# The bias of the attention's exponentials, 24 small products, on Pool instead of DVE

## The chip, the cores and the metric

The kernel runs on one core of a Trainium2 chip. A core has a matrix engine (TensorE; PE in the profile, its weight loads PEld), a vector engine (VectorE; DVE), a scalar engine (ScalarE; ACT), a general engine (GpSimd; Pool, or POOL) and a queue that issues transfers (SyncE; SP). Each works off its own list of instructions in the order in which they were issued, and waits where one needs a result of another engine. The metric is the device time of one execution in microseconds; the kernel before takes 1005.35 us, the median of three runs (1005.01 to 1005.65).

## The reference

The reference is a decoder of two layers over 256 tokens of width 1024, in float32. Each layer is half a SwiGLU feed-forward block, a mixer and another half block, each on a normalised input and added to the stream. The mixer of the first layer is a short gated convolution; that of the second is sparse attention with 16 heads of 64 in 4 groups, in three branches (compressed, selected, window) that share one set of keys and values. At 256 tokens there are only four blocks of 64, so every block is selected, and the selected branch and the window branch are plain causal attention with keys of their own:

```
logits = einsum("bghtd,bgtkd->bghtk", qc, ks) * scale
p_sel  = softmax(where(smask, logits, -1e30))
o_sel  = einsum("bghtk,bgtkd->bghtd", p_sel, vs)
logits = einsum("bghtd,bgkd->bghtk", qc, kw) * scale
p_win  = softmax(where(wmask, logits, -1e30))
out    = gc[0] * o_cmp + gc[1] * o_sel + gc[2] * o_win
```

Queries are normalised per head with a learned gain, gates are sigmoids. Nearly all of the arithmetic is in the eight big weight products of the four feed-forward blocks.

## The kernel before, in words

The stream h lies transposed in SBUF, features on partitions. All weights come in float32 through one queue into three buffers `raw`; ScalarE rounds each to `whi`, VectorE (for a few units Pool) computes the rest `wlo = raw - whi`, and TensorE multiplies with both. Units of such work follow one another: feed-forward, convolution, feed-forward, shared keys and values, feed-forward, attention, feed-forward.

In the attention (`nsa`), 24 steps, called heads below, run through six rounds `U` of four: a round is a pair of query tile and half, and each head makes a 128 x 512 tile of logits `S` for both branches (`qk`). For one head the chain is:

- TensorE writes S in PSUM (weights are the scaled keys `kth` and `kts`, with the mask added by a product with `identb`).
- VectorE takes the negated maxima `mx` of S, 2 or 4 groups per row (lines 1168 and 1172).
- `nb = mx * sc` is the bias of the exponentials, 128 x 2 or 128 x 4 elements; `sc` is the query's scale, which Pool made before by a power (`q_stat`, line 1082).
- ScalarE computes `P = exp(sc * S + nb)` in 2 or 4 instructions, with row sums (line 1180).
- VectorE inverts the sums (`pw`), Pool multiplies them with the gates, and then P (128 x 512) by them (`weight`, lines 1187 to 1196).
- TensorE transposes P into `pb` (`tr`, two banks of `psB`), ScalarE rounds it to `ph`, VectorE makes the rest `pl`, and TensorE multiplies both with the values into `pc` (`pv`), which VectorE and ScalarE add up in `t`.

`mx` and `nb` are tiles of the pool `work`, with two buffers each, so that those of a head reuse the place of those of two heads before. S has four banks. Between these steps stand the compressed branch (`cm`, `mc`), the last query projections (`S<-hg,whi`, `qs`) and, from the middle on, the output projection `wo` of the first half.

The order in which each engine gets its instructions isn't that of the code. `Plan` records all operations with their dependences, gives each a cost (`_cost`; a small product on `gp` costs more there than one on `ve`) and a lag between engines (`LATENCY`), and a list scheduler (`schedule`, `sweep`) makes one order for each engine, four passes back and forth; `replay` then issues all of it, which is why the profile names line 419 for every instruction. A change of one operation's engine so changes costs and lags, and the order around it.

Of the kernel before, what the change touches and what calls it, by code (L numbers as in the profile page):

```python
# [15 lines left out]
ALU = mybir.AluOpType  # L16
# [415 lines left out]
def program(plan, a, out, ones):  # L432
    pe, ac, ve, gp, sp = (Engine(plan, k, None) for k in ("pe", "act", "dve", "gp", "sp"))
# [22 lines left out]
    def tt(eng, o, x, y, op):  # L456
        eng.tensor_tensor(o, x, y, op)
# [584 lines left out]
    def nsa(nkey, gname, okey, ogains):  # L1042
        st = {}
# [28 lines left out]
        def q_stat(i):  # L1072
            if i in st["stats"]:
                return
            st["stats"].add(i)
            t = psC.tile([128, 2, 2], F32, name="pc")
            for q in range(2):
                pe.matmul(t[:, q], st["sq", i][:, q * 128:(q + 1) * 128], blk2, start=True, stop=True)
            x = work.tile([128, 2, 2], F32, name="s8")
            ve.scalar_tensor_tensor(x, t, 1.0 / 64, st["em"][:, :, None].to_broadcast([128, 2, 2]),  # L1080
                                    op0=ALU.mult, op1=ALU.add)
            tt(gp, st["sc", i // 4][:, i % 4], x, neghalf[:, :, None].to_broadcast([128, 2, 2]), ALU.pow)
# [63 lines left out]
        def qk(i, hh):  # L1146
            j, q, ab = U[i]
            if hh % 2 == 0:
                P[i, hh // 2] = st["pool"].tile([128, 2, 4, 128], F32, name="P", bufs=5)
            if hh == 0:  # L1150
                SUM[i] = work.tile([128, 4, 4], F32, name="psum_")
            S = wide["pool"].tile([128, 512], F32, name="S")
            for x in range(2):
                e, y, k = (ab, hh, x) if q else (hh // 2, hh % 2 * 2 + x, 0)
                q_stat(j * 4 + y)
                qs = st["qs", j * 4 + y, e][:, q * 128:(q + 1) * 128]
                Sx = S[:, x * 256:(x + 1) * 256]
                Sb = Sx.rearrange("p (a b) -> p a b", a=2)
                pe.matmul(Sb, qs, kth[k][e][:, :, j], start=True, stop=False)
                if k == q:  # L1160
                    pe.matmul(Sx, identb, mask2, start=False, stop=False)
                pe.matmul(Sb, qs, kts[k][e][:, :, j], start=False, stop=True)
            g = 2 if q else 4
            mx = work.tile([128, 4], F32, name="mx")[:, :g]
            nb = work.tile([128, 4], F32, name="nb")[:, :g]
            if q:
                Sv = S.rearrange("p (k b c) -> p b k c", b=2, k=2)
                ve.tensor_reduce(mx, Sv, axis=AX.XY, op=ALU.max, negate=True)
                tt(ve, nb, mx, st["sc", j][:, hh, q, ab:ab + 1].to_broadcast([128, 2]), ALU.mult)
            else:  # L1170
                Sv = S.rearrange("p (x b c) -> p x b c", x=2, b=2)
                ve.tensor_reduce(mx, S.rearrange("p (g c) -> p g c", g=4), axis=AX.X, op=ALU.max, negate=True)
                tt(ve, nb.rearrange("p (x b) -> p x b", b=2), mx.rearrange("p (x b) -> p x b", b=2),
                   st["sc", j][:, hh % 2 * 2:hh % 2 * 2 + 2, q, hh // 2, None].to_broadcast([128, 2, 2]), ALU.mult)
            for y in range(g):
                if q:
                    o, x, z, e = P[i, hh // 2][:, hh % 2, 2 * y:2 * y + 2], Sv[:, y], hh, ab
                else:
                    o, x, z, e = P[i, hh // 2][:, hh % 2, y], Sv[:, y // 2, y % 2], hh % 2 * 2 + y // 2, hh // 2
                ac.activation(o, x, AF.Exp, bias=nb[:, y:y + 1], scale=st["sc", j][:, z, q, e:e + 1],  # L1180
                              accum_out=SUM[i][:, hh, y:y + 1])
# [113 lines left out]
        def attention():  # L1295
# [26 lines left out]
            for n in range(max(events) + 1):  # L1322
                st["head"] = n
                if n < len(heads):
                    if n == 12:
                        assert st["qdone"]
                    qk(*heads[n])
                    yield
                if 1 <= n <= len(heads):
                    weight(*heads[n - 1])  # L1330
                for f, args in sorted(events.get(n, []), key=lambda e: e[0] is not pv):
                    f(*args)
                    yield
# [92 lines left out]
    for u, x, y in HEAD:  # L1426
        if u == "h":
            x, y = NPAR * (x > 0) + x * T, NPAR + y * T
# [141 lines left out]
```

## Time and profile before

| | |
|---|---|
| time, median of 3 | 1005.35 us (1005.01 to 1005.65) |
| profiled execution | 1006.19 us, span 1004.4 us |
| mean granted clock of TensorE | 0.998 of full speed |
| busy PE / PEld | 983.8 us (98%) / 859.4 us (86%) |
| busy DVE / ACT / POOL | 734.3 us (73%) / 586.1 us (58%) / 203.2 us (20%) |
| chain that ended last | PE 85%, DVE 7%, ACT 3%, issue 2%, POOL 2% |
| heads of the attention | first `mx` at 724.6 us, last `nb` at 778.0 us |

The page counts an engine as busy while one of its instructions runs; the chain that ended last follows back, from the end, what each instruction waited for. Times in rows are counted from the start of the span. All instructions of the attention have the same line, so they are told apart by the names of the tiles: `nb<-mx,sc` writes nb from mx and sc.

### The profile page before, as it was taken

The page shows a single profiled execution, that of the slowest core. Times are in us where ns is not written, and L with a number is a line of the kernel's source. Part 1 is how long each engine was busy: PE and PEld are TensorE (multiplying, and loading weights), DVE is VectorE, ACT ScalarE, POOL GpSimd, SP SyncE. Part 2 cuts the span into 40 slices and gives each one's busy share as a digit, 9 for nine tenths or more (in the row PEclk, how much of TensorE's full clock was granted, in tenths as well). Part 3 has the DMA queues.
Part 4 walks back from the last instruction along what each step waited for, and adds up shares of the span by engine and source line. Part 5 has one row for each costly group of instructions (what it writes and reads, how often), then busy time and mean ns, then how long its engine had stood idle before and what let it go on. Part 6 is the DMA issues. An engine that isn't in the chain of part 4 may idle for free.

```text
span 1004.4 us, 15242 instructions
## 1 busy us (share of the span) xinstructions
PE 983.8 (98%) x5792; PEld 859.4 (86%) x5792; DVE 734.3 (73%) x1110; ACT 586.1 (58%) x1049; POOL 203.2 (20%) x242
## 2 busy tenths in 40 slices
PE   8999999999999999999899999999998999999998
PEld 5888888888888888889778888888986888888887
DVE  6876766688796767677989776676799787676554
ACT  8665554454565555554687565554698765555442
POOL 2211111022221111111421111111477431111100
PEclk9999999999999999999999999999999999999999
DMA  8655455655565554557366554455510245554353
GB/s 281 236 204 176 162 173 181 210 175 186 206 209 181 196 186 153 173 193 264 132 212 226 196 205 165 138 200 192 197 43 11 93 174 186 192 185 156 128 198 107
DMA packets 31033, 177.83 MB, mean 177 GB/s; under 512 B 3440, under 2 KB 6000, under 8 KB 16112
## 3 DMA queue, kind: packets, MB, share of 16 engines
q1 hardware_dynamic: 30960, 176.86, 51.4%
q8 instruction: 45, 0.74, 0.3%
q14 instruction: 28, 0.23, 0.1%
HBM read 175.80 MB, written 1.05 MB: 176 GB/s over the span
## 4 chain that ended last, share of the span: by engine, by line
PE 85%; DVE 7%; ACT 3%; issue 2%; POOL 2%; DMA 1%; SPq 1%; ACTq 0%; DVEq 0%; POOLq 0%
PE pa L419 52%; PE pb L419 29%; PE S L419 2%; PE pc L419 2%; DVE wlo L419 2%; ACT whi L419 1%; DVE mx L419 1%; DVE hg L419 1%; DVE nb L419 1%; DMA px<-in_px_dram 1%; DVE pl L419 1%; SPq L419 1%; DVE px L419 1%; POOL rf L419 0%; DVE t L419 0%
## 5 line engine op out<-in xcount | busy, mean ns | idle before, releaser
L419 PE MATMUL pa<-hg,whi 128*128 128x512 f32 (+1 forms) x1568 | 538.9, 390 | 2.9 <-DVE hg L419 2.7
L419 DVE TENSOR_TENSOR wlo<-raw,whi 128x1024 fp32r<-128x1024 f32 (+4 forms) x383 | 412.3, 1092 | 164.2 <-ACT whi L419 162.7
L419 ACT CAST whi<-raw 128x1024 fp32r<-128x1024 f32 (+3 forms) x388 | 350.6, 927 | 196.2 <-issue 80.9
L419 PE MATMUL pa<-hg,wlo 128*128 128x256 f32 x1536 | 430.8, 281 | 0.1
L419 PEld LDWEIGHTS pa<-hg,whi 128*128 128x128 f32 x1568 | 291.6, 187 | 68.8 <-DVE hg L419 4.5
L419 PEld LDWEIGHTS pa<-hg,wlo 128*128 128x128 f32 x1536 | 290.3, 189 | 0.9 <-DVE wlo L419 0.7
L419 PE MATMUL pb<-gg,whi 128*128 128x512 f32 x704 | 244.1, 392 | 0.0
L419 PE MATMUL pb<-gg,wlo 128*128 128x256 f32 x704 | 195.6, 279 | 0.0
L419 PEld LDWEIGHTS pb<-gg,whi 128*128 128x128 f32 x704 | 131.6, 187 | 29.4
L419 POOL TENSOR_TENSOR g<-s,t 128x256 f32<-128x256 f32 x88 | 70.3, 799 | 414.3 <-ACT s L419 410.4
L419 PEld LDWEIGHTS pb<-gg,wlo 128*128 128x128 f32 x704 | 132.7, 188 | 0.3
L419 ACT ACTIVATE s<-t 128x256 f32<-128x256 f32 x88 | 36.8, 418 | 138.3 <-DVE t L419 138.3
L419 POOL TENSOR_TENSOR acc<-acc,sq 128x256 f32<-128x256 f32 x36 | 33.5, 932 | 177.6 <-ACT sq L419 177.0
L419 DVE TENSOR_TENSOR t<-pa,t 128x512 f32<-128x512 f32 x94 | 64.3, 684 | 3.6 <-ACT t L419 3.4
L419 DVE TENSOR_TENSOR t<-t,R 128x512 f32<-128x512 f32 x96 | 66.2, 689 | 0.1
L419 ACT COPY t<-pa 128x512 f32<-128x512 f32 x94 | 54.5, 579 | 2.8 <-PE pa L419 2.6
L419 PE MATMUL S<-hg,whi 128*128 128x256 f32 (+1 forms) x224 | 49.2, 302 | 1.8 <-DVE hg L419 1.3
L419 DVE SCALAR_TENSOR_TENSOR px<-pb,px 128x256 f32<-128x256 f32 x56 | 23.7, 423 | 34.3 <-PE pb L419 33.4
L419 PE MATMUL pb<-hg,whi 128*128 128x512 f32 (+1 forms) x144 | 48.2, 386 | 0.0
L419 DVE TENSOR_TENSOR gg<-g,gg 128x256 fp32r<-128x256 f32 x88 | 37.2, 424 | 12.2 <-ACT gg L419 12.2
L419 ACT CAST gg<-g 128x256 fp32r<-128x256 f32 x88 | 35.4, 403 | 13.6 <-POOL g L419 12.5
L419 DVE SCALAR_TENSOR_TENSOR hg<-px,hg 128x256 fp32r<-128x256 f32 x56 | 39.6, 726 | 2.2 <-ACT hg L419 2.1
(176 smaller groups left out, 879.9 us busy)
## 6 DMA issues: line engine op xcount, KB each, us to landing
raw<-in_wgu_dram SPq DMA_DIRECT2D x86, 1024.0 KB, 4.8
raw<-in_wdn_dram SPq DMA_DIRECT2D x64, 704.0 KB, 4.1
raw<-in_wci_dram SPq DMA_DIRECT2D x8, 1024.0 KB, 5.0
raw<-in_wci_dram SPq DMA_DIRECT2D x8, 512.0 KB, 3.6
raw<-in_wco_dram SPq DMA_DIRECT2D x4, 1024.0 KB, 4.7
raw<-in_wkt_dram SPq DMA_DIRECT2D x4, 1024.0 KB, 4.8
raw<-in_wc_dram SPq DMA_DIRECT2D x4, 1024.0 KB, 4.9
raw<-in_wq_dram SPq DMA_DIRECT2D x4, 1024.0 KB, 4.8
```

Of the source, the lines that this page charges most:

```text
L419: getattr(engines[op.eng], op.name)(*[real(x) for x in op.args], **{k: real(v) for k, v in op.kw.items()})
```

## The change

The product `nb = mx * sc` is issued to `gp` (Pool) instead of `ve` (VectorE), at both places of `qk`; its operands and its shape stay.

```
-                tt(ve, nb, mx, st["sc", j][:, hh, q, ab:ab + 1].to_broadcast([128, 2]), ALU.mult)
+                tt(gp, nb, mx, st["sc", j][:, hh, q, ab:ab + 1].to_broadcast([128, 2]), ALU.mult)
...
-                tt(ve, nb.rearrange("p (x b) -> p x b", b=2), mx.rearrange("p (x b) -> p x b", b=2),
+                tt(gp, nb.rearrange("p (x b) -> p x b", b=2), mx.rearrange("p (x b) -> p x b", b=2),
```

With it the planner's order changes within the attention on every engine but the transfer queue, which keeps its order. Two places are shown. A number behind a name tells instances of a tile apart; it isn't the same before and after.

First VectorE at the tenth, eleventh and twelfth head, before:

```order
L419 TENSOR_REDUCE mx_7322<-S_7296 128x2
L419 RECIPROCAL pw_7334<-psum__7173 128x2
L419 TENSOR_TENSOR pl_7336<-pb_7258,ph_7317 128x512
L419 TENSOR_TENSOR nb_7347<-mx_7322,sc0_6817 128x2
L419 RECIPROCAL mc_7293<-mc_7293 128x16
L419 RECIPROCAL pw_7354<-psum__7327 128x2
L419 TENSOR_REDUCE mx_7358<-S_7331 128x2
L419 TENSOR_TENSOR t2_7349<-t2_7349,pc_7276 64x512
L419 TENSOR_TENSOR nb_7381<-mx_7358,sc0_6817 128x2
L419 RECIPROCAL pw_7384<-psum__7327 128x2
L419 TENSOR_REDUCE mx_7387<-S_7369 128x2
```

The same heads on VectorE now:

```order
L419 TENSOR_REDUCE mx_7305<-S_7292 128x2
L419 RECIPROCAL pw_7317<-psum__7176 128x2
L419 TENSOR_TENSOR pl_7327<-pb_7258,ph_7314 128x512
L419 RECIPROCAL pw_7338<-psum__7296 128x2
L419 TENSOR_REDUCE mx_7343<-S_7324 128x2
L419 TENSOR_TENSOR t2_7322<-t2_7322,pc_7280 64x512
L419 RECIPROCAL pw_7364<-psum__7296 128x2
L419 TENSOR_REDUCE mc_7367<-cm_7154 128x16
L419 TENSOR_TENSOR pl_7375<-pb_7268,ph_7359 128x512
L419 SCALAR_TENSOR_TENSOR s8_7387<-pc_7276,em_6793 128x4
L419 TENSOR_REDUCE mx_7391<-S_7362 128x2
```

And the same heads on Pool now, where nb of each stands ahead of P and pw of an earlier head:

```order
L419 TENSOR_TENSOR nb_7331<-mx_7305,sc0_6817 128x2
L419 TENSOR_TENSOR pw_7317<-pw_7317,gates_6924 128x2
L419 TENSOR_TENSOR P_7236<-P_7236,pw_7317 128x512
L419 TENSOR_TENSOR nb_7356<-mx_7343,sc0_6817 128x2
L419 TENSOR_TENSOR pw_7338<-pw_7338,gates_6924 128x2
L419 TENSOR_TENSOR P_7295<-P_7295,pw_7338 128x512
L419 TENSOR_TENSOR pw_7364<-pw_7364,gates_6924 128x2
L419 TENSOR_TENSOR sc1_7122<-s8_7387,neghalf_83 128x4
L419 TENSOR_TENSOR nb_7412<-mx_7391,sc0_6817 128x2
```

VectorE has lost its nb from between the maxima, and Pool's list has gained one per head.

Second, Pool at the rest of the first weights of `wo` (`wlo`, 128 x 1024). Before, it stood among the last heads, when their P were being multiplied:

```order
L419 TENSOR_TENSOR P_7670<-P_7670,pw_7708 128x512
L419 TENSOR_TENSOR pw_7750<-pw_7750,gates_6924 128x2
L419 TENSOR_TENSOR wlo_7304<-raw_6908,whi_7281 128x1024
L419 TENSOR_TENSOR P_7670<-P_7670,pw_7750 128x512
L419 TENSOR_TENSOR pw_7768<-pw_7768,gates_6924 128x4
```

Now it stands between nb of the sixteenth and of the seventeenth head:

```order
L419 TENSOR_TENSOR nb_7502<-mx_7486,sc1_7122 128x2
L419 TENSOR_TENSOR P_7389<-P_7389,pw_7460 128x512
L419 TENSOR_TENSOR nb_7536<-mx_7497,sc1_7122 128x2
L419 TENSOR_TENSOR wlo_7437<-raw_6908,whi_7409 128x1024
L419 TENSOR_TENSOR nb_7583<-mx_7533,sc1_7122 128x2
L419 TENSOR_TENSOR cm_7546<-cm_7546,sc1_7122 128x256
```

Pool's largest instruction of the attention has moved ahead of eight nb; the last weights' rest and the last heads no longer meet.

## Rows read from the trace of the kernel before

**Rows 1.** Stretches: busy time of PE, PEld, DVE, ACT, POOL; clock; DMA

```profile
725.00:742.00 17.00, 17.00 (x143) 16.26 (x143) 14.63 (x38) 16.19 (x60) 10.96 (x17) 1.00 0.22 75
742.00:778.00 36.00, 29.96 (x203) 25.25 (x202) 33.51 (x80) 31.23 (x95) 26.75 (x42) 0.95 0.03 5
...
750.00:760.00 10.00, 9.21 (x56) 7.87 (x55) 7.99 (x20) 7.94 (x24) 6.17 (x9) 0.83 0.00 0
...
770.00:780.00 10.00, 7.38 (x45) 5.26 (x43) 9.16 (x20) 8.44 (x29) 9.49 (x14) 1.00 0.27 94
```

**Rows 2.** The chain that ended last, from 744 to 779 us, by line

```profile
by line: DVE mx L419 18.0%; DVE nb L419 15.4%; issue 13.9%; PE pc L419 13.2%; PE S L419 9.7%; DVE pl L419 8.7%; PE pb L419 7.2%; DVE t L419 5.9%; DVE cm L419 2.9%; DVE pw L419 2.5%; DVE qs L419 2.5%; DVE mc L419 0.6%; DVE wlo L419 0.6%; DVE
```

**Rows 3.** Groups by form from 715 to 805 us: busy us, mean ns, idle

```profile
L419 DVE TENSOR_TENSOR nb<-mx,sc 128x2 f32<-128x2 f32 x16 | 5.5, 345 | 0.2
L419 DVE TENSOR_TENSOR nb<-mx,sc 128x4 f32<-128x4 f32 x8 | 4.1, 518 | 0.1
L419 POOL TENSOR_TENSOR pw<-pw,gates 128x2 f32<-128x2 f32 x16 | 3.4, 215 | 4.4 <-DVE pw L419 4.4
```

**Rows 4.** The tile nb: shortest, median and longest of one, in ns

```profile
L419 DVE TENSOR_TENSOR nb<-mx,sc x24: 146/196/1492, 725.8 to 778.0; 128x2 f32<-128x2 f32 x16, 128x4 f32<-128x4 f32 x8
```

**Rows 5.** Timeline of DVE: start us, us, what

```profile
746.94 0.99 DVE L419 TENSOR_TENSOR nb<-mx,sc 128x2 f32<-128x2 f32 x1
...
750.71 0.80 DVE L419 TENSOR_TENSOR nb<-mx,sc 128x2 f32<-128x2 f32 x1
751.54 0.43 DVE L419 TENSOR_TENSOR qs<-S,qs 64x256 fp32r<-64x256 f32 x1
...
769.87 0.63 DVE L419 TENSOR_TENSOR nb<-mx,sc 128x4 f32<-128x4 f32 x1
...
771.19 0.84 DVE L419 TENSOR_TENSOR nb<-mx,sc 128x4 f32<-128x4 f32 x1
...
774.74 1.49 DVE L419 TENSOR_TENSOR nb<-mx,sc 128x4 f32<-128x4 f32 x1
...
776.24 0.65 DVE L419 TENSOR_TENSOR pl<-pb,ph 128x512 fp32r<-128x512 f32 x1
```

**Rows 6.** Timeline of POOL at two of these

```profile
746.87 1.04 POOL L419 TENSOR_TENSOR P<-P,pw 128x512 f32<-128x512 f32 x1
...
773.86 2.35 POOL L419 TENSOR_TENSOR wlo<-raw,whi 128x1024 fp32r<-128x1024 f32 x1
```

**Rows 7.** Timeline of PE: its waits, in brackets, and what ended them

```profile
749.28 0.39 PE L419 MATMUL S<-kth,qs 128*128 128x256 f32 x1 [1.51 <-ACT P L419]
...
752.02 0.58 PE L419 MATMUL S<-kth,qs 128*128 128x256 f32 x1 [0.79 <-DVE qs L419]
...
773.38 0.63 PE L419 MATMUL pb<-cst,P 128*128 128x128 f32 x4 [0.46 <-DVE pl L419]
...
774.96 0.63 PE L419 MATMUL pb<-cst,P 128*128 128x128 f32 x4 [0.73 <-DVE pl L419]
...
776.95 0.66 PE L419 MATMUL pb<-cst,P 128*128 128x128 f32 x4 [1.36 <-DVE pl L419]
```

**Rows 8.** Timeline of DVE, POOL and ACT: hops from engine to engine

```profile
748.01 0.10 DVE L419 RECIPROCAL pw<-psum__7327 128x2 f32<-128x2 f32 x1
...
748.19 0.20 POOL L419 TENSOR_TENSOR pw<-pw,gates 128x2 f32<-128x2 f32 x1 [0.28 <-DVE pw L419]
...
748.02 0.56 ACT L419 ACTIVATE P<-S,nb,sc 128x256 f32<-128x256 f32 x1 [1.88 <-DVE nb L419]
...
777.16 0.21 POOL L419 TENSOR_TENSOR pw<-pw,gates 128x4 f32<-128x4 f32 x1
...
777.48 0.46 ACT L419 ACTIVATE P<-S,nb,sc 128x128 f32<-128x128 f32 x1 [0.35 <-POOL pw L419]
```

**Rows 9.** POOL's waits from 742 to 778 us: total, times, longest

```profile
POOL pw L419 <- DVE pw L419: 4.4, 6, 1.4
POOL cm L419 <- DVE nb L419: 2.7, 1, 2.7
```

## The prediction

> **What bounds the kernel now.** The page is read first: TensorE is busy almost everywhere, so a change on VectorE and Pool can only tell where TensorE idles. Next come stretches of the attention, the one part that the change touches. In [rows 1] the reader sees two regimes. From 725 to 742 us TensorE is busy for all of 17.00 us: the query projections fill every gap, and no small product decides anything. From 742 to 778 us it is busy for 29.96 of 36.00 us, while VectorE has 33.51, ScalarE 31.23 and Pool 26.75. TensorE has run out of other work there, and the latency of the heads sets the time. The chain of waits over about this stretch (744 to 779 us) is the third view [rows 2]: nb alone takes 15.4% of it, 0.154 x 35 = 5.4 us, as the second line after mx.
>
> That is odd for so small an instruction, so the groups by form and the tile come fourth [rows 3, 4]. The 24 nb cost VectorE 5.5 + 4.1 = 9.6 us, though the shortest takes 0.146 us. At 0.15 us each they would take 3.6 us; the other 6.0 us are stalls inside the instruction. The timelines show with what: the nb that starts at 774.74 and takes 1.49 us ends at 776.23, and Pool's wlo of 2.35 us ends at 776.21; the nb of 746.94 ends at 747.93, and Pool's P of 1.04 us ends at 747.91 [rows 5, 6]. These two stood still on VectorE until Pool's running instruction was done, and the others of [rows 5] are read the same way.
>
> The Trainium skill (SBUF — State Buffer, "SBUF: two separate sides") names a cause: VectorE and GpSimd share one pair of ports as an exclusive lock, and a VectorE instruction with two SBUF inputs blocks fully while a GpSimd one holds it. The two endings above agree to 0.02 us. By that rule all 6.0 us leave VectorE and only wlo and one product of the compressed branch could still be blocked there; the sum below doesn't count them in full, since the instruction meets the same Pool work again, in its queue.
>
> **The change part by part.** *Removed from VectorE:* 24 nb, 9.6 us busy. Of this only what TensorE waited for is time. TensorE's waits that follow a long nb are in [rows 7]. (a) Before 749.28 it waits 1.51 us for P, whose exponentials start at 748.02 after ScalarE had waited 1.88 us for the nb of 0.99 us [rows 8]; the nb's own excess, 0.99 - 0.15 = 0.84 us, is what goes. (b) Before 752.02 it waits 0.79 us for qs, which starts right behind the nb of 0.80 us: 0.80 - 0.15 = 0.65 us. (c) Before 773.38, 774.96 and 776.95 it waits 0.46 + 0.73 + 1.36 = 2.55 us for pl, which stands behind the nb of 0.63, 0.84 and 1.49 us on VectorE (the last pl starts at 776.24, as the nb ends); their excess is 2.96 - 0.45 = 2.51 us. Sum: 0.84 + 0.65 + 2.51 = 4.0 us gained. What is late next behind these waits is ScalarE's list: 31.23 of 36 us allow no more than 4.8 us, so the 4.0 us fit barely.
>
> *Added to Pool:* 24 small products. Pool's product of a 128 x 2 tile, pw, takes 0.215 us [rows 3], the nearest row there is, so 24 x 0.215 = 5.2 us in all and 16 x 0.215 = 3.4 us in the 36 us. Pool has 36.00 - 26.75 = 9.25 us free there, but from 770 to 780 us only 10.00 - 9.49 = 0.51 us, and four nb come in: 4 x 0.215 = 0.86, so 0.35 us overflow if nothing moved. The planner moved wlo, 2.35 us, out of just this place, so I take 0 to 0.35 us, and count 0.3.
>
> The Trainium skill (GPSIMD Engine Reference, "Performance versus the Vector engine") speaks against the move: VectorE stays the choice for elementwise work, with GpSimd 1.96 times slower on a two-input product. By that, as an estimate, an nb would take 0.29 us and Pool's addition in the 36 us 4.6 us instead of 3.4; the row's 0.215 us, 1.5 times VectorE's shortest, decides here, and the sum would lose about 0.2 us more.
>
> *A longer way per head:* before, nb (0.15 us) and its hop to ScalarE (747.93 to 748.02, 0.09 us). Now a hop to Pool (748.11 to 748.19, 0.08 us), 0.21 us, and a hop to ScalarE (777.37 to 777.48, 0.11 us) [rows 8]. That is 0.40 - 0.24 = 0.16 us more for each head whose exponentials are awaited. None is awaited before 742 us; of the 16 heads after it ScalarE had room to wait about a third, so 5 x 0.16 = 0.8 us, with bounds of 0 and 2.6.
>
> *Moved waits:* nb on Pool stands behind whatever Pool runs, so for the exponentials the stall stays. At 746.94 this costs no more than before, since the nb now stands ahead of the P that held it up. The trace of before doesn't show Pool waiting for mx, with P of an earlier head queued behind. From below it is nothing (the maximum is there, as VectorE is earlier), from above one P, 1.04 us [rows 6], for each of the last 8 heads, 8.3 us. Nothing moves these together, and Pool's waits for VectorE get shorter; I take 0.4 us, near the lower end. The re-planned order of the projections from 725 to 742 us lies beside a full TensorE: nothing, from -1 to +1 us by the hops.
>
> Sum: -4.0 + 0.3 + 0.8 + 0.4 = -2.5 us. Against the profiled execution, 1006.19 us, that gives 1003.7 us; that execution lay 0.84 us above the median, and at the median's level the forecast is 1005.35 - 2.5 = 1002.85, taken as 1002.8 us.
>
> **The rivals.** *More than the sum.* From 750 to 760 us the granted clock is 0.83 [rows 1], so about a third of the stretch ran at 1.2 GHz; the two waits of [rows 7] before 752.02 lie ahead of it. If they vanish and the clock stays, up to half of 3.4 us, 1.7 us, comes back besides the 4.0 us, and the rest of the chain's 5.4 us may follow: 5.7 us with few costs, 999.6 us. For it: the chain runs through TensorE just there. Against: other waits remain in the round.
>
> *No difference.* ScalarE's list, 31.23 of 36.00 us, is the next limit: each exponential still waits for Pool's running instruction, and TensorE's waits change their name from pl and qs to P. Then (b) and (c) are mostly given back and about 0.5 us is left: 1004.8 us. For it: the wait (a) already came through ScalarE. Against: pl and qs, which freed TensorE's banks, don't depend on nb.
>
> *Slower: Pool becomes the bound.* mx and nb have two buffers, so the maximum of a head waits until the nb of two heads before is done, and that nb now lies in Pool's list. Where Pool lags, VectorE's maxima stop, and pl behind them. The place is from the sixteenth head on, where wlo (2.35 us, and it first awaits a cast on ScalarE) stands ahead of nb, cm and P. Pool's busy 26.75 us, its waits for VectorE of 4.4 + 2.7 us [rows 9] and the 3.4 us added are 37.3 us, 1.3 us more than 36; one wlo in the way of an nb adds 2.35 us minus what the two buffers cover, 0.6 us or so for one small step: +3.0 us, 1008.4 us. It decides from the point at which Pool's waits in the stretch stay above 9.25 - 3.4 = 5.85 us. For it: 4.4 + 2.7 is above that now. Against: both waits are for VectorE, which has 7 us less to do there, and the 2.7 us one ended on an nb.
>
> **How the numbers follow.** A difference under 0.2%, 2.0 us, counts as none. The forecast, a gain of 2 to 5 us around 1002.8, gets 0.40, with a range of its own from 1000.4 to 1003.3; more than that 0.10; no difference 0.22; slower 0.28, since three engines are coupled more tightly and the order is new over 60 us. Faster is so 0.50, within the bound 0.22, slower 0.28. The range reaches from 998.5 us, below the larger gain, to 1008.4 us, the slower case; it leaves out half of the slower case and little at the low end.
>
> **What would show each step.** In the changed kernel's trace: VectorE without nb, busy near 26 us in the 36 us (or however long the stretch is), and pl right behind its ph; the 24 nb on Pool at 0.2 us each, none above 0.3; TensorE's waits for pl and qs behind the eighth head gone, 4 us less in total; the dip of the clock smaller or absent. The stretch from the first mx to the last exponential should shrink by 2 to 3 us and all after it begin earlier by that. I am wrong if ScalarE's waits for POOL nb total over 4 us, if VectorE's mx waits for POOL nb, or if TensorE waits for P where it waited for pl. The forecast also fails if the stretch is shorter but the units of the output projection after it wait as much more.

## The result, and the profile after

The changed kernel takes 1001.13 us, the median of four runs (999.55 to 1002.02), against 1005.5 us for four of the kernel before (1005.01 to 1007.05): 4.4 us less between the medians. The ratio of all executions is 0.9947, 95% interval 0.9934 to 0.9959, so 0.5% or 5.3 us faster by the ratio. Two repeats on other chips gave 0.996 [0.9944, 0.9976] and 0.9952 [0.993, 0.9973], which is 4.0 and 4.8 us. The profiled execution took 1002.02 us with a span of 1000.2, against 1006.19 and 1004.4 before.

The stretches of [rows 1], in the same columns, in the changed kernel:

```profile
725.00:742.00 17.00, 17.00 (x148) 16.52 (x147) 13.59 (x30) 16.18 (x58) 11.69 (x24) 1.00 0.26 94
742.00:778.00 36.00, 33.44 (x222) 27.63 (x222) 30.65 (x70) 35.51 (x112) 32.27 (x63) 0.95 0.09 30
...
770.00:780.00 10.00, 8.53 (x44) 6.49 (x42) 6.38 (x15) 9.95 (x34) 8.96 (x17) 0.83 0.00 1
```

TensorE is idle for 36.00 - 33.44 = 2.56 us where it was idle for 6.04. ScalarE is now the busiest engine, with 35.51 of 36.00 us; whether it is also the bound is asked in an experiment below. One wider window takes in the whole slack stretch and what follows it, here of the kernel before:

```profile
742.00:820.00 78.00, 70.67 (x468) 61.20 (x467) 68.04 (x145) 61.67 (x156) 45.45 (x59) 0.98 0.19 64
```

And of the changed one:

```profile
742.00:820.00 78.00, 75.10 (x497) 65.29 (x497) 65.69 (x134) 64.69 (x164) 49.21 (x77) 0.98 0.22 74
```

TensorE's idle time falls from 7.33 to 2.90 us, by 4.43; the span falls by 4.2. So the gain lies here and nothing of it is lost later. The last exponential's sum is read until 785.03 us before and until 780.15 after; from the first mx on (724.59 and 723.97 us) that is 60.4 and 56.2 us.

The chain of waits over 742 to 776 us, by line, answers to [rows 2]:

```profile
by line: ACT P L419 27.7%; PE pc L419 16.0%; ACT ph L419 8.5%; PE S L419 7.6%; DVE mx L419 7.3%; PE pb L419 6.2%; DVE pl L419 5.6%; ACT t L419 5.1%; issue 4.8%; POOL nb L419 3.6%; DVE qs L419 2.1%; DVE cm L419 1.8%; POOL mc L419 1.0%; ACT c
```

nb has gone from 15.4% to 3.6%, and ScalarE's exponentials lead. The groups by form answer to [rows 3]:

```profile
L419 POOL TENSOR_TENSOR nb<-mx,sc 128x2 f32<-128x2 f32 x16 | 4.1, 258 | 1.0 <-ACT P L419 0.8 <-DVE mx L419 0.2
L419 POOL TENSOR_TENSOR nb<-mx,sc 128x4 f32<-128x4 f32 x8 | 2.5, 307 | 1.5 <-DVE mx L419 1.4
```

And the tile of nb to [rows 4], the shortest, median and longest in ns:

```profile
L419 POOL TENSOR_TENSOR nb<-mx,sc x24: 187/197/1213, 724.8 to 773.8; 128x2 f32<-128x2 f32 x16, 128x4 f32<-128x4 f32 x8
```

The median is 0.197 us, where the prediction had 0.215 from the row of pw and 0.29 by the ratio of 1.96, but the longest is 1.21. What TensorE still waits for between 742 and 778 us, against [rows 7]:

```profile
758.66 0.63 PE L419 MATMUL pb<-cst,P 128*128 128x128 f32 x4 [0.35 <-DVE pw L419]
760.07 0.50 PE L419 MATMUL pc<-ph,vhl 128*128 128x512 f32 x1 [0.16 <-ACT ph L419]
763.73 0.63 PE L419 MATMUL pb<-cst,P 128*128 128x128 f32 x4 [0.29 <-DVE pl L419]
764.53 0.38 PE L419 MATMUL S<-kth,qs 128*128 128x256 f32 x1 [0.17 <-ACT P L419]
772.01 1.22 PE L419 MATMUL pb<-cst,P 128*128 128x128 f32 x8 [1.47 <-DVE pl L419]
```

Of the wait of 1.51 us for P, 0.17 is left, and the one of 0.79 us for qs is gone. TensorE's waits for pl are best counted over the wide window, 715 to 820 us (total, times, longest), first before and then in the changed kernel:

```profile
PE pb L419 <- DVE pl L419: 4.4, 6, 1.4
...
PE pb L419 <- DVE pl L419: 1.8, 2, 1.5
```

Of the six waits for pl before, [rows 7] has three. One of the others, 1.02 us before 766.58, lies in the stretch as well, but the nb ahead of it took only 0.35 us; the other two come after 778 us.

### The profile page after: what moved, and what is told of

Its sections match the earlier page's. It is cut to its first block, busy times and chain, and to the rows that moved or that the text cites. A ratio compares the mean times of both kernels' runs of the same rounds, so it can differ in the third digit from the quotient of the medians.

```text
span 1000.2 us, 15237 instructions
## 1 busy us (share of the span) xinstructions
PE 985.0 (98%) x5792; PEld 859.4 (86%) x5792; DVE 727.5 (73%) x1086; ACT 585.7 (59%) x1049; POOL 207.9 (21%) x266
## 4 chain that ended last, share of the span: by engine, by line
PE 88%; DVE 4%; ACT 4%; issue 1%; POOL 1%; DMA 1%; SPq 0%; ACTq 0%; DVEq 0%; POOLq 0%
PE pa L419 52%; PE pb L419 29%; PE S L419 4%; PE pc L419 3%; DVE wlo L419 1%; ACT P L419 1%; ACT whi L419 1%; DVE hg L419 1%; DMA raw<-in_wgu_dram 1%; DVE px L419 0%; POOL rf L419 0%; DMA px<-in_px_dram 0%; ACT kth L419 0%; DVE s L419 0%; POOL hg L419 0%
```

## The experiments

Two things change at once: the engine of nb, and the order into which the planner then puts the attention. *The stall theory* says that nb stood still on VectorE behind Pool, and that this is what was gained. *The order theory* says that the new order does it, wherever nb runs. In several kernels below the planner plans as in one kernel and nb is issued on another engine or in another form; all other instructions then keep that kernel's order. Line numbers shift by one to four. All ratios are to runs of the kernel before on the same chip, and a gain in us is worked out from the ratio, so it can differ from that of the medians by up to a microsecond. Code is shortened.

### The new order, nb on VectorE

```
 tt(gp, nb, mx, ...)                       # planned as the changed kernel
+plan.ops[-1].emit = "dve"                 # issued on VectorE
```

> The order of every engine is that of the changed kernel, but nb is issued to VectorE at its place in that order; nothing else differs. Theory A (the gain is that VectorE no longer stands still while Pool's instruction runs): the stalls are back, VectorE's 24 nb take 7 to 11 us together, and the time is near that of the kernel before, 1004 to 1006 us. Rival B (the gain is the planner's new order, whichever engine does the product): 1000.5 to 1002 us.

Measured: 1004.05 us, ratio 0.9968 [0.9955, 0.9982], 3.2 us faster. So the order without the move gives most of the gain. The busy time of nb alone shows how (columns: the window, VectorE and ScalarE, which reads nb). Before:

```profile
742.00:782.00 40.00, 7.58 (x17) 22.06 (x76) 0.96 0.08 27
```

In this experiment:

```profile
742.00:782.00 40.00, 4.08 (x16) 24.32 (x86) 1.00 0.08 27
```

And its tile:

```profile
L420 DVE TENSOR_TENSOR nb<-mx,sc x24: 132/233/849, 725.4 to 775.8; 128x2 f32<-128x2 f32 x16, 128x4 f32<-128x4 f32 x8
```

The 742 to 782 us hold 4.08 us of nb instead of 7.58: in the stretch in which TensorE idles, the new order itself avoids most of the stalls. Over the whole attention the 24 nb take 7.8 us instead of 9.6, as the stall theory expected; the rest of them lie before 742 us. A reason can be that the planner had set time on Pool aside for each nb, in which Pool now has nothing to run; no run isolates it. So the two theories meet here: the order works through the same stalls. As a separate cause it was not yet ruled out.

### The order before, nb on Pool

```
 tt(ve, nb, mx, ...)                       # planned as the kernel before
+plan.ops[-1].emit = "gp"                  # issued on Pool
```

> The order of every engine is that of the kernel before, but nb is issued to Pool at its place in that order. Theory A: the 24 nb take 4 to 7 us on Pool, VectorE has none, and most of the gain is there without the new order, 1001 to 1003.5 us. Rival B: near the kernel before or slower, 1005 to 1007 us, since nb is queued behind P products that the old order put ahead of it.

Measured: 1002.99 us, ratio 0.9957 [0.9944, 0.997], 4.3 us faster: the move without the order gives all of it, within the intervals. The stretch:

```profile
742.00:778.00 36.00, 32.47 (x228) 27.08 (x226) 30.95 (x70) 34.32 (x108) 31.53 (x62) 1.00 0.03 6
```

The tile of nb:

```profile
L420 POOL TENSOR_TENSOR nb<-mx,sc x24: 196/199/381, 727.7 to 777.1; 128x2 f32<-128x2 f32 x16, 128x4 f32<-128x4 f32 x8
```

And ScalarE's waits for it in the whole attention (715 to 801 us; total, times, longest):

```profile
ACT P L420 <- POOL nb L420: 2.0, 3, 1.3
```

nb is hardly held up on Pool here, but ScalarE waits for it for 2.0 us (three times, 1.3 the longest). In the changed kernel's own order this wait is 0.6 us; so the new order saves 1.4 us of ScalarE's waits, which the times can't tell from nothing.

### The order before, 16 nb with one tensor operand

If only the second tensor operand made VectorE stand still, nb with the scale as a per-partition scalar would run freely. This changes the 16 nb of two columns.

```
-tt(ve, nb, mx, st["sc", j][...].to_broadcast([128, 2]), ALU.mult)
+ve.tensor_scalar(nb, mx, st["sc", j][:, hh, q, ab:ab + 1], None, op0=ALU.mult)
```

> The kernel before, in its own order, with the 16 nb of 128 x 2 issued on VectorE as a tensor times a per-partition scalar, so that only one operand is a tensor; the 8 nb of 128 x 4 stay. Theory A in its narrow form (it is the second tensor operand in SBUF that makes VectorE stand still): these 16 take about 0.15 to 0.2 us each, 3 us less than the 5.5 us before, and the waits before 749 and 752 us shrink: 1003.0 to 1004.3 us. Rival C (any small VectorE instruction meets the stall, or a form with a scalar meets it too): their total stays above 4.5 us and the time within 0.5 us of before.

Measured: 1006.19 us, ratio 0.9997 [0.998, 1.0014]: nothing gained. VectorE's group:

```profile
L419 DVE TENSOR_SCALAR nb<-mx,sc 128x2 f32<-128x2 f32 x16 | 6.2, 391 | 0.2
```

An instruction of it, and Pool's beside it, from the timelines:

```profile
747.29 0.99 DVE L419 TENSOR_SCALAR nb<-mx,sc 128x2 f32<-128x2 f32 x1
...
747.22 1.04 POOL L419 TENSOR_TENSOR P<-P,pw 128x512 f32<-128x512 f32 x1
```

The stretch:

```profile
742.00:778.00 36.00, 29.98 (x208) 25.13 (x207) 34.81 (x82) 31.41 (x96) 27.69 (x44) 0.99 0.05 16
```

The stall is as it was: nb ends at 748.28, Pool's P at 748.26. In this instruction one tensor and a per-partition scalar in SBUF are enough, even with two columns. The narrow form of the theory fell; the stall itself is confirmed. The stretch shows the clock at 0.99 where the kernel before had 0.95, but the dip lies elsewhere here: from 770 to 780 us the clock is 0.85.

### The order before, nb with an operand in PSUM

A form that reads one tensor from PSUM, on VectorE, with nothing on Pool:

```
+op = plan.ops[-1]
+op.name, op.args, op.kw = "scalar_tensor_tensor", (nb, S[:, :g], 0.0, mx), {"op0": ALU.mult, "op1": ALU.add}
```

> The order of every engine is that of the kernel before and nb stays on VectorE, but it is made by an instruction with one tensor from PSUM (S times 0.0) plus the one from SBUF (mx); left out are the product with the query's scale and the scale of the exponentials, which take a column of ones. Theory A (VectorE's stand-still behind Pool, which needs both tensors, or a tensor and a scalar, in SBUF): each of the 24 takes 0.15 to 0.25 us, none over 0.4, about 5 us together, and the time is 1001 to 1003 us with nothing on Pool and no new order. Rival E (what counts is that VectorE has one instruction less per head, or Pool's order): 24 instructions still stand there, and the time stays within 1 us of before. If the stalls remain in this form, theory A's narrow form falls and the time is that of before.

Measured: 1000.08 us, ratio 0.9944 [0.9922, 0.9966], the whole gain. The stretch:

```profile
742.00:778.00 36.00, 33.40 (x235) 27.85 (x233) 32.37 (x89) 35.43 (x110) 30.15 (x48) 1.00 0.09 30
```

The tile:

```profile
L419 DVE SCALAR_TENSOR_TENSOR nb<-S,mx x24: 139/158/164, 727.4 to 774.5; 128x2 f32<-128x2 f32 x16, 128x4 f32<-128x4 f32 x8
```

The longest of 24 takes 0.164 us. The engine is the same, the order is that of before, the stall is gone, and the gain is there. That this nb has no scale to wait for is a second difference, so the form was tried again with the scale in it.

### The same with nothing left out, in both orders

```
-tt(ve, nb, mx, sc...)
+scalar_tensor_tensor(nb, mx, sc[:, hh, q, ab:ab + 1], S[:, :2], op0=ALU.mult, op1=ALU.bypass)
```

Heads with two scales take two such instructions, 32 in all. In the order before:

> Nothing is left out here: the order of the kernel before, nb on VectorE, made exactly, as mx times the scale as a per-partition scalar with a second tensor from PSUM (S) that the instruction reads and passes by; where a head has two scales, it takes two such instructions. Theory A: as with the PSUM form before, no instruction of nb over 0.3 us, 32 of about 0.16 us; 1000.5 to 1002 us, level with the changed kernel or up to 1 us below it. If the form with a scalar from SBUF stands still whatever the second tensor is, its instructions reach 1 us and the time is that of before.

Measured: 1000.77 us, ratio 0.9953 [0.9929, 0.9977], on the chip where the changed kernel had 1000.76 and 0.9952. A tie. The wide window:

```profile
742.00:820.00 78.00, 74.38 (x499) 64.38 (x498) 67.97 (x154) 63.68 (x161) 45.78 (x60) 1.00 0.24 82
```

The tile:

```profile
L421 DVE SCALAR_TENSOR_TENSOR nb<-mx,sc,S x32: 201/211/218, 725.0 to 772.8; 128x2 f32<-128x2 f32 x32
```

Each takes about 0.21 us, not the expected 0.16, and none over 0.218. From the timelines of VectorE and Pool:

```profile
770.18 0.34 DVE L421 SCALAR_TENSOR_TENSOR nb<-mx,sc,S 128x2 f32<-128x2 f32 x2
...
769.59 2.37 POOL L423 TENSOR_TENSOR wlo<-raw,whi 128x1024 fp32r<-128x1024 f32 x1
```

Two nb of this form run in 0.34 us in the midst of Pool's wlo (769.59 to 771.96), just what one took 1.49 us for in [rows 5]. In the changed kernel's order:

> The same exact form on VectorE, in the order of the changed kernel. If order and freedom from stalls add up, this is the fastest, 999 to 1000.5 us; if the new order gains only by keeping nb and Pool's instructions apart, there is nothing left for it to do, and the time is within 1 us of the old order with the same form.

Measured: 1002.07 us, ratio 0.9971 [0.9956, 0.9986]. The tile:

```profile
L421 DVE SCALAR_TENSOR_TENSOR nb<-mx,sc,S x32: 189/211/218, 727.1 to 775.9; 128x2 f32<-128x2 f32 x32
```

TensorE's longest waits from 715 to 820 us:

```profile
PE pb L423 <- DVE pl L423: 2.1, 2, 1.7
```

With no stall left, the new order isn't better than the old one, 2.9 us against 4.7: it gains nothing of its own. It still has a wait of 1.7 us of TensorE for pl. The intervals overlap, so neither order is shown to be better. The order theory, apart from the stalls, falls.

### Is ScalarE the next bound?

The changed kernel with eight copies of pc moved from ScalarE to VectorE, planned anew:

```
-ac.copy(o, OH[i][64:128])
+ve.tensor_copy(o, OH[i][64:128])
```

> The changed kernel, with the 8 copies of 64 x 512 from pc to t (0.58 us each on ScalarE) issued to VectorE, re-planned. Theory A goes on: in the changed kernel ScalarE is busy for 35.51 of the 36.00 us from 742 to 778 us and is now the bound; 8 x 0.58 = 4.6 us less there, of which about half lie in that stretch, should give 1 to 2.5 us: 998.7 to 1000.2 us. Rival D (another engine or the chain of one head bounds it as closely): within 0.6 us of the changed kernel, or slower by the 0.6 us that VectorE's copy adds to each round.

Measured: 1004.26 us, ratio 0.9971 [0.9958, 0.9983]: a miss, nothing better than the changed kernel. The stretch:

```profile
742.00:778.00 36.00, 32.36 (x227) 27.24 (x226) 33.98 (x73) 33.71 (x102) 33.17 (x61) 1.00 0.16 59
```

ScalarE's waits for nb in the whole attention:

```profile
ACT P L419 <- POOL nb L419: 2.8, 4, 1.2
```

ScalarE has room again, 33.71 us, and waits longer for nb than in the changed kernel. VectorE, ScalarE and Pool are within 0.81 us of each other. So easing ScalarE at VectorE's expense doesn't help, and that ScalarE alone is the bound isn't shown.

### Do the two buffers of mx and nb, or Pool's list, cost anything?

The changed kernel with four buffers for both, and another with the six wlo of the output projection taken off Pool and planned anew:

```
-bufs=t.bufs
+bufs=4 if t.name in ("mx", "nb") else t.bufs
...
-CQ, CO, PQ, PO = 0, 0, 6, 6
+CQ, CO, PQ, PO = 0, 0, 6, 0
```

> The changed kernel in its own order, with four buffers instead of two for mx and nb. The slower rival of the prediction rests on these two buffers (a maximum waits for the nb of two heads before, on Pool, and that one for the exponentials of two heads before). If this coupling costs anything in the changed kernel, Pool's wait of nb for ACT P (0.8 us in three places) goes and 0.3 to 1 us with it; if it costs nothing, the time is within 0.5 us of the changed kernel.

> The changed kernel, re-planned, with the rests of the output projection's weights (wlo, 2.4 us a half on Pool) all on VectorE, where a half takes 1.2 us. Pool is busy for 32.27 of the 36.00 us from 742 to 778 us in the changed kernel; without wlo it has 29.9, VectorE 31.9 instead of 30.65. If Pool's list is near the bound, 0.5 to 2 us are gained; if ScalarE alone bounds the stretch (35.51 of 36), it is within 0.6 us; if VectorE's wlo meets Pool's instructions and stands still, 0.5 to 1.5 us slower.

The four buffers gave 1003.46 us, ratio 0.9979 [0.9964, 0.9995]; on the same chip the unchanged repeat gave 0.996, and the intervals overlap. nb no longer waited for ScalarE's P, and the last exponential began at 779.5 us, as in the repeat; from 724 to 820 us TensorE is busy for 92.47 us here and 92.37 in the repeat. So in the trace the coupling costs nothing. The median is 1.8 us higher, which neither branch of the expectation allowed, and this isn't explained. Without wlo on Pool: 1001.97 us, ratio 0.9963 [0.995, 0.9977], no change, with Pool's load down:

```profile
742.00:778.00 36.00, 33.81 (x237) 28.14 (x236) 32.81 (x74) 35.21 (x109) 29.92 (x61) 1.00 0.09 31
```

Pool at 29.92 us instead of 32.27 brings no time, with VectorE at 32.81 instead of 30.65 in exchange, so nothing here shows Pool as the bound.

### The changed kernel again

> The changed kernel once more, beside the next three on one chip: 4 to 5.5 us below the kernel before.

> The changed kernel beside the next two on one chip: 4 to 5.5 us below the kernel before.

Measured: 1001.64 against 1005.66 us, and 1000.76 against 1005.15 us. The trace of the first answers one more question:

```profile
742.00:778.00 36.00, 32.72 (x222) 26.37 (x220) 30.64 (x70) 35.52 (x112) 32.28 (x63) 1.00 0.09 30
770.00:780.00 10.00, 7.79 (x44) 5.33 (x42) 6.44 (x15) 9.95 (x36) 8.96 (x17) 1.00 0.00 1
```

The dip of the clock to 0.83 from 770 to 780 us is absent here, and the span is 1000.2 us with it and without it. TensorE's busy time is 0.72 us less, and its idle time as much more.

## Why the prediction was right, and where its terms were off

The forecast was 1002.8 us, 2.5 us under the median before; measured 1001.13, a gain of 4.4. The sign, the mechanism and the forecast's own range held.

**What was removed.** The gross term of 4.0 us was right in its sum and only partly in its parts. TensorE's wait (a), for P, fell by 1.34 us where the prediction took off 0.84, and wait (b), for qs, by 0.79 where it took off 0.65. The waits for pl fell by 2.6 us where (c) took off 2.51; but (c) rests on three waits of 2.55 us, and it is six waits of 4.4 us that became two, of 1.47 and 0.29 us. New waits, for pw and ph, cost 0.5 us. That the sum came out near 4.0 is in part luck. The wait that is left, 1.47 us, has this before it on VectorE:

```profile
770.58 0.69 DVE L419 TENSOR_REDUCE mx<-S 128x4 f32<-128x512 f32 x1 [1.13 <-PE S L419]
771.18 1.28 DVE L419 TENSOR_TENSOR pl<-pb,ph 128x512 fp32r<-128x512 f32 x2
```

ScalarE's first cast to ph is done at 770.56 us, but pl stands in VectorE's list behind a maximum that had waited 1.13 us for TensorE's S, and the chain of waits runs through S, mx and pl there. So behind this wait it is S and the order on VectorE that are late next, and not ScalarE's list, as the prediction put it; on the rest of the chain ScalarE's exponentials do lead. That the stall on VectorE was the cause of the gain is shown: with the order before, nb without the stall gives the gain on Pool (4.3 us) and on VectorE (4.7), and where the stall stays (the scalar form) there is none.

**Which cause the stall has.** The Trainium skill (SBUF — State Buffer, "SBUF: two separate sides") counts among what is locked out by GpSimd not only two SBUF inputs, on which the prediction rested, but also any VectorE operation in a two-port mode. The traces agree with the first half: nb with both tensors in SBUF stands still up to 1.49 us, and the forms of nb with a tensor in PSUM never take above 0.218. The scalar form, with one tensor in SBUF, stands still up to 0.99 us, which the second half allows; which port mode an instruction ran in, no row here shows, so that half isn't shown. Its sentence that the lock works both ways agrees with the rows under the last heading; the prediction didn't price that.

**The costs were what was mis-sized**: 0.3 + 0.8 + 0.4 = 1.5 us were taken off, and little of it was lost. *The longer way*, 0.8 us: ScalarE waits for POOL nb for 0.6 us at one exponential and 0.3 us at one other instruction, in the whole attention. The step that failed is "ScalarE had room to wait about a third": it was busy for 35.51 of 36.00 us, nearly always had something queued, and nb was done ahead of it. What nb still takes on the chain, 3.6% or 1.2 us, is one nb of 1.21 us that VectorE's wlo held up on Pool (last heading), which the prediction priced at nothing. In the order before, the same hop does cost ScalarE 2.0 us. *Moved waits*, 0.4 us: VectorE's mx waits for PE alone, never for nb, and POOL nb waits for ScalarE's P 0.8 us in all, and with four buffers, without these waits, the last exponential begins no earlier. *Pool's overflow*, 0.3 us: from 770 to 780 us Pool is busy for 8.96, not over 10.

**Of what would show it:** "VectorE busy near 26 us" was wrong; it has 30.65, since the 36 us now hold some 4 us of later work, which a fixed window can't tell apart. The prediction's "one product of the compressed branch could still be blocked there" held: `cm<-cm,mc`, with both tensors in SBUF, went from 0.42 to 1.02 us in the mean of its two instances. "The 24 nb on Pool at 0.2 us each" held for the median, "none above 0.3" didn't: two took over a microsecond. The stretch shrank by 4.2 us, not 2 to 3. The dip of the clock was as deep in the changed kernel's profiled execution (0.83) and absent in its repeat. Of the three signs of failure, ScalarE's waits for nb stayed under 4 us and mx never waited for it; no long wait for P took the place of one for pl.

**The rivals.** *More than the sum* came near in size (5.7 us against 4.4) but not by its mechanism. At the same mean granted clock, 0.998, the kernel before takes 1004.77 us (mean of 15 executions) and the changed one 1000.61 (6) on the chip of the first repeat, and 1004.65 (15) and 1000.33 (4) on that of the second: 4.2 and 4.3 us less. The changed kernel's executions at 1.0 are no faster (1001.77 and 1001.07 us). So the gain doesn't hang on the clock. *No difference* named the engine that is busiest afterwards, ScalarE, but its 31.23 us left the room for the gain. *Pool becomes the bound* didn't come about: Pool is busy for 32.27 of 36.00 us, and neither less work for it nor more buffers brought time.

**What stays open.** Why the new order without stalls (1002.07 us) lies above the order before without stalls (1000.77) was not followed beyond the 1.7 us wait for pl; their intervals overlap. What bounds the attention now stays open too: neither easing ScalarE nor easing Pool at VectorE's expense gained time. No version that computes all of nb was clearly faster than the changed kernel.

## What to carry to other kernels

A stall inside an instruction shows as busy time: compare the shortest, median and longest of a small instruction, and where they lie far apart look for the engine whose instruction ends with it. Before moving such an instruction off VectorE, try a form with a tensor operand in PSUM; here it gave the same gain without loading Pool. Price a longer way between engines only where the receiving engine has nothing else queued.

## What the runs showed of the hardware

The lock works the other way too. In the changed kernel VectorE's wlo, started first, holds Pool's nb:

```profile
750.79 1.20 DVE L419 TENSOR_TENSOR wlo<-raw,whi 128x1024 fp32r<-128x1024 f32 x1
...
750.84 1.21 POOL L419 TENSOR_TENSOR nb<-mx,sc 128x2 f32<-128x2 f32 x1 [0.20 <-DVE mx L419]
```

They end at 751.99 and 752.05 us, and the nb is six times its median. On VectorE, a small size doesn't protect an instruction: the scalar form of nb, two columns with all operands in SBUF, took 0.391 us in the mean against 0.214 for its shortest, while the form with the same tile, the same scalar and a third operand in PSUM stayed between 0.189 and 0.218 us in 64 instructions, whatever Pool ran. But not every VectorE instruction meets the stall. In the changed kernel, Pool's P and two that start on VectorE while it runs:

```profile
768.17 1.04 POOL L419 TENSOR_TENSOR P<-P,pw 128x512 f32<-128x512 f32 x1
...
768.31 0.15 DVE L419 RECIPROCAL pw<-psum__7596 128x2 f32<-128x2 f32 x1
768.38 0.67 DVE L419 TENSOR_TENSOR pl<-pb,ph 128x512 fp32r<-128x512 f32 x1
```

The reciprocal of two columns, whose only tensor lies in SBUF (`psum_` is the name of a tile there), took 0.11 to 0.17 us in all 16 instances of this trace. pl is the operation of nb, TENSOR_TENSOR, with one tensor (pb) in PSUM, and took 0.67 to 0.69 us in all 24. So it is not the operation alone that decides, and one tensor in SBUF is not always enough.
